# Low parts of split weights made by a negating copy and an accumulating transfer instead of a VectorE subtraction

## The chip, the core and the metric

The kernel runs on one core of a Trainium2 chip. A core has five engines that run at the same time, each with its own queue of instructions that it takes in order: TensorE (PE in the profile; its weight loads are PEld), VectorE (DVE), ScalarE (ACT), GpSimd (POOL) and SyncE (SP), which here only issues DMA transfers. Sixteen DMA engines move data between DRAM and the on-chip memory. The metric is the device time of one execution in microseconds (us); the median of three runs of the kernel before is 1519.1 us (1518.18 to 1520.67).

## What is computed

One block of a streaming encoder on 512 tokens of 1024 features, in float32: two SwiGLU feed-forwards around a mixer, and a last norm.

```python
x = x + 0.5 * swiglu(rms_norm(x, n1), ffn1_w_in, ffn1_w_out)      # 1024 -> 2*2816 -> 1024
h = rms_norm(x, nm)
b, c, xa, z, xbc, dt, ga, gb = split(h @ w_in)
y_a = (b * conv3(c * xa)) @ short_w_out
xs, bm, cm = split(silu(conv4(xbc) + bias))                       # 32 heads in 8 groups
y_b = group_norm((ssd_scan(xs, dt, bm, cm) + xs * D) * silu(z)) @ ssm_w_out
x = x + (sigmoid(ga) * y_a + sigmoid(gb) * y_b) @ w_out
x = x + 0.5 * swiglu(rms_norm(x, n2), ffn2_w_in, ffn2_w_out)
return rms_norm(x, nf)
```

Nearly all the arithmetic is in the matrix products with the weights. Their precision comes from splitting each factor into two float32r numbers, a high part and a low part.

## The kernel before

**Blocks of weights.** All weights are read once from DRAM, as 260 blocks in the order of their use (`src`, lines 82 to 107). A block has 128 partitions and as a rule 8 K-tiles of 128 columns (1024 float32 values in each partition, 512 KB); the third block of each output tile of a feed-forward has 6 K-tiles, the three blocks `wz0` of the first group have 3, 3 and 2 K-tiles of 288 columns.

**prep()** (lines 110 to 127) makes the next block ready. SP loads it into a tile `wraw` (two buffers, line 121). ScalarE copies `wraw` to `wh`, rounding to float32r: the high part (line 125). VectorE subtracts `wh` from `wraw` into `wl`: the low part (line 126). `wh` and `wl` have three buffers each.

**take()** (line 131) gives the oldest ready block to its user and calls prep() for one more, so that two blocks are being prepared or stand ready while one is in use. A block's `wh` and `wl` go into the buffers of the block three before it, so its preparation can't begin before TensorE has finished with that block.

**The main stream.** `mm3` (line 158) multiplies a block with the activations, which are split as well: for each K-tile three matmuls, high weights with high activations (line 164), high with low (165), low with high (166). The low part of a block is thus first needed by its third matmul. TensorE's order is written out by hand: after each K-tile `sq.tick()` puts in the small matmuls of the mixer that are due (class Order). The order on the other engines is left to the Tile framework, which also places all semaphores.

**Stages.** First feed-forward: 44 blocks of input weights, 24 of output weights. Mixer: 8 groups. A group projects C (a block), then B and two blocks x0, x1 (each followed by a convolution on VectorE and SiLU on ScalarE, `conv_silu`, line 369, which begins with a small memset on GpSimd, L371), and z through `gate` (line 301), which keeps its blocks for four token tiles: in group 0 the three blocks `wz0`, in the others two blocks at the end of the group. The first group also has the chain for dt (`dt_chain`, line 337) on VectorE. The scan of a group puts many small operations on all engines: `steps` (GpSimd, L471), `weights` (matmul L480, exp L483, VectorE L484), `within` (L493), `states` (matmul L453, VectorE L460 and L463), `across` (L504), the gated norm (L515 to L529, with GpSimd L510 and L527). Matmul L409 is the first one of `inner`, once in each group. Then come the merge gates, the SSD output projection, the short convolution, its projection, `w_out`, and the second feed-forward. The last output tile of all is done in two halves of the tokens (lines 679 to 692), so that its six blocks are each used for half the usual time, and the norm of the first half runs beside the second half's products.

Of the kernel before, what the change touches and what calls it, by code (L numbers as in the profile page):

```python
# [12 lines left out]
F32 = mybir.dt.float32  # L13
F32R = mybir.dt.float32r
AF = mybir.ActivationFunctionType
ALU = mybir.AluOpType
# [13 lines left out]
NC = T // P  # L30
EPS = 1e-5

# columns of the packed per-feature parameters
PF_N1, PF_NM, PF_N2, PF_NF = 0, 8, 16, 24
PF_SC = 32
PF_CW = 56
# [3 lines left out]


class Order:
    """The order of the tensor engine's work: the main stream advances in ticks (a K-tile of a
    projection each); what depends on other engines is put in so many ticks later."""

    def __init__(self):
        self.now = 0
# [22 lines left out]
def hybrid_block(ctx: ExitStack, tc: tile.TileContext, xT, w1i, w1o, wmx, wz0, wso, wsso,  # L70
# [7 lines left out]
    ctx.enter_context(tc.manual_schedule(engines={mybir.EngineType.PE}))  # L78
    sq = Order()

# [1 line left out]
    src = []  # L82
    src += [(w1i[i], KT) for i in range(2 * FT)]
    kcut = [(0, 8), (8, 16), (16, FT)]
# [23 lines left out]
    ready = []  # L108

    def prep():  # L110
        """The next block of weights as two float32r parts whose sum is exact."""
        if not src:
            return
        ap, _ = src.pop(0)
        n = ap.shape[-1]
        raw = wp.tile([P, D], F32, tag="wraw", name="wraw", bufs=2)
        cuts = [slice(0, n)]
        if len(src) == NSRC - 1:
            cuts = [slice(0, n // 2), slice(n // 2, n)]
        for h in cuts:  # L120
            nc.sync.dma_start(raw[:, h], ap[:, h])
        wh = wp.tile([P, D], F32R, tag="wh", name="wh")
        wl = wp.tile([P, D], F32R, tag="wl", name="wl")
        for h in cuts:
            nc.scalar.copy(wh[:, h], raw[:, h])  # L125
            nc.vector.tensor_tensor(wl[:, h], raw[:, h], wh[:, h].bitcast(F32), ALU.subtract)  # L126
        ready.append((wh, wl))

    NSRC = len(src)
# [3 lines left out]
        prep()  # L133
        return w

# [1 line left out]
    xall = pers.tile([P, KT, T], F32, name="xall")  # L137
    xr = [xall[:, j, :] for j in range(KT)]
    pf = pers.tile([P, PF_W], F32, name="pf")
# [11 lines left out]
    def col(i):  # L151
        return pf[:, i : i + 1]

# [1 line left out]
    def bank(tag="mm"):  # L155
        return ps.tile([P, T], F32, tag=tag, name=tag, bufs={"mm": 3, "sg": 2}.get(tag, 1))

    def mm3(out, w, xs, first=True, last=True, tk=slice(0, T)):
        """out += w.T @ x over the K-tiles xs, both in pairs of parts, for the tokens tk."""
        wh, wl = w  # L160
        n = len(xs)
        for i, xk in enumerate(xs):
            sl = slice(i * P, (i + 1) * P)
            nc.tensor.matmul(out, wh[:, sl], xk[:, 0, tk], start=first and i == 0, stop=False)  # L164
            nc.tensor.matmul(out, wh[:, sl], xk[:, 1, tk], start=False, stop=False)  # L165
            nc.tensor.matmul(out, wl[:, sl], xk[:, 0, tk], start=False, stop=last and i == n - 1)  # L166
            sq.tick()
# [9 lines left out]
        nc.vector.tensor_tensor(dst[:, 1, :], s, dst[:, 0, :].bitcast(F32), ALU.subtract)  # L177

    class Norm:
        """RMS norm of the residual: the parts of x * gain, and 1 / RMS per token, which the  # L180
        products are scaled by afterwards."""

        def __init__(self, gain):
            self.gain = gain
# [85 lines left out]
                nc.scalar.activation(xr[m], xr[m], AF.Copy, scale=col(PF_NF + m))  # L270
        return hid

# [1 line left out]
    n1 = Norm(PF_N1)  # L274
    prep()
    n1.parts(0)
# [17 lines left out]
    ffn(n1, nm, ("mm", "mm", "mm", "py", "po", "tr"))  # L294
    nm.later(5, 11)

# [1 line left out]
    xw = nm.xw  # L298
    CH = NC * HEADS

    def gate(zw, wide, c0, cn):
        """z of a group for the token blocks c0 .. c0 + cn, tokens on the partitions."""
        pz = bank()
        for c in range(c0, c0 + cn):
            o = pz[:, (c - c0) * wide : (c - c0 + 1) * wide]
            tk = slice(c * P, (c + 1) * P)
            step = -(-KT // len(zw))
            for k in range(KT):
                wh, wl = zw[k // step]
                sl = slice(k % step * wide, (k % step + 1) * wide)  # L310
                nc.tensor.matmul(o, xw[k][:, 0, tk], wh[:, sl], start=k == 0, stop=False)  # L311
                nc.tensor.matmul(o, xw[k][:, 0, tk], wl[:, sl], start=False, stop=False)  # L312
                nc.tensor.matmul(o, xw[k][:, 1, tk], wh[:, sl], start=False, stop=k == KT - 1)  # L313
                if k % 2 == 1:
                    sq.tick()
        return pz
# [18 lines left out]
                                       pr[:, 0:HEADS], ALU.mult, ALU.add)  # L335

    def dt_chain():
        # softplus(v) = max(v, 0) + log1p(exp(-|v|)), log1p(e) = 2 atanh(e / (2 + e))
        nc.vector.scalar_tensor_tensor(e, v, -1.0, v, ALU.mult, ALU.min)
        nc.scalar.activation(e, e, AF.Exp)  # L340
        na = tp.tile([P, HEADS], F32, tag="na", name="na", bufs=1)
        nc.scalar.activation(na, pr[:, HEADS : 2 * HEADS], AF.Exp)
        nc.vector.tensor_scalar(s, e, 2.0, None, ALU.add)
        nc.vector.reciprocal(s, s)
        nc.vector.tensor_tensor(s, s, e, ALU.mult)
        nc.vector.tensor_tensor(s2, s, s, ALU.mult)
        nc.vector.tensor_scalar(pl, s2, 2.0 / 17, 2.0 / 15, ALU.mult, ALU.add)
        for q in (13, 11, 9, 7, 5, 3, 1):
            nc.vector.tensor_tensor(pl, pl, s2, ALU.mult)
            nc.vector.tensor_scalar(pl, pl, 2.0 / q, None, ALU.add)  # L350
        nc.vector.tensor_tensor(pl, pl, s, ALU.mult)
        nc.vector.scalar_tensor_tensor(dt, v, 0.0, pl, ALU.max, ALU.add)
        nc.vector.scalar_tensor_tensor(av, dt, -1.0,
                                       na.unsqueeze(1).broadcast_to([P, NC, HEADS]),
                                       ALU.mult, ALU.mult)
        nc.vector.tensor_copy(ah, av)
        nc.vector.tensor_tensor(al, av, ah.bitcast(F32), ALU.subtract)

    def decays():
        """exp of the sums of a within a chunk: up to a token, after it, and of all."""  # L360
        pe = bank("sg")
        for i, m in enumerate((tri, mgt_r.bitcast(F32), ones)):
            nc.tensor.matmul(pe[:, i * CH : (i + 1) * CH], m, av.rearrange("p c h -> p (c h)"),
                             start=True, stop=True)
        nc.scalar.activation(dec.rearrange("p i c h -> p (i c h)"), pe[:, : 3 * CH], AF.Exp)
        nc.vector.tensor_tensor(dtd, dt, ds, ALU.mult)

    def conv_silu(o, pt, ft):
        """Scale, causal convolution over 4 taps, bias and SiLU of one 128-channel tile."""
        xp = tp.tile([P, T + 3], F32, tag="ta", name="xp")  # L370
        nc.gpsimd.memset(xp[:, 0:3], 0.0)  # L371
        nc.vector.tensor_tensor(xp[:, 3:], pt, nm.rb, ALU.mult)
# [11 lines left out]
        return act.tile(shape, dtype, tag="act", name=name, bufs=FT)  # L384

    class Group:
        """One group of the SSD mixer: 4 heads that share B and C."""

        def __init__(self, g):
            self.g = g  # L390
# [5 lines left out]
            self.st = [None] * NC  # L396

        def heads(self, apx):
            """Values of the group's heads, each over its 64 channels."""
            n = apx.shape[1]  # L400
            return apx[:, :, self.hs].unsqueeze(3).broadcast_to([P, n, HG, HD])

        def inner(self):
            """C B^T within the chunks, [s, l], and B with tokens on the partitions."""
            pc = bank("sg")
            pb = bank("tr")
            for c in range(NC):
# [40 lines left out]
                ALU.mult)  # L448

        def states(self, c):  # L450
            """State that enters chunk c + 1: what chunk c adds and the decayed one before."""
            pst = bank("po")
            nc.tensor.matmul(pst[:, :GC], self.btk[:, c, :], self.xdd[:, c, :],  # L453
                             start=True, stop=True)
# [9 lines left out]
            self.st[c + 1] = sn  # L464

        def steps(self, c):
            """a of chunk c masked to the tokens up to l, [t, head, l], in two parts."""
            self.au[c] = []
            for part in (ah.bitcast(F32), al):
                au = tp.tile([P, HG, P], F32R, tag="td", name="au", bufs=3)  # L470
# [3 lines left out]
                self.au[c].append(au)  # L474

        def weights(self, c):
            """exp(sum of a over (s, l]) * C B^T of chunk c, [s, head, l]."""
            sgp = bank("sg")
            for i in range(2):
                nc.tensor.matmul(sgp, mgt_r, self.au[c][i].rearrange("p h l -> p (h l)"),  # L480
# [5 lines left out]
            self.ex[c] = ex  # L486

        def within(self, c):
            # two heads wide: head h's part lies at 128 h, the last one's at 128 h + 64
            py = bank("py").rearrange("p (h l) -> p h l", l=P)  # L490
            for h in range(HG):
                d0 = min(h * HD, GC - P)
# [88 lines left out]
                pz = gate(zw, GC, c0, 2)  # L581
                gate_out(pz, G.zs, GC, c0, 2)

    # gates of the merge, then the SSD output projection
    mb = []
    for j in range(KT):
        pt = project(xw)
# [15 lines left out]
            mm3(pt, take(), ys[i * KT : (i + 1) * KT], i == 0, i == 1)  # L603
        nc.vector.tensor_tensor(mb[m], pt, mb[m], ALU.mult)

    # short gated convolution
    ya = []
    for j in range(KT):
        pc = project(xw)
# [39 lines left out]
        n2.parts(m)  # L649
        n2.square(m)  # L650

# [1 line left out]
    n2.later(5, 11)  # L653
    nf = Norm(None)
    hid = ffn(n2, None)
    # the last feature tile in halves of the tokens: the first half's norm and output run
    # beside the second half's products
    m = KT - 1
    nf.last = tp.tile([P, T], F32, tag="td", name="nlast", bufs=3)

# [32 lines left out]


def blocks(w, mw=P):
    """[K, M] -> [M / mw, P, K / P * mw]: the K-tiles of each block of mw columns side by side."""
    k, m = w.shape
    return w.reshape(k // P, P, m // mw, mw).transpose(2, 1, 0, 3).reshape(m // mw, P, k // P * mw)


def feat(v):
    """[n, F] per-feature rows -> [P, F / P * n], feature tile by feature tile."""
    n, f = v.shape
    return v.reshape(n, f // P, P).transpose(2, 1, 0).reshape(P, f // P * n)

# [52 lines left out]
```

## Time and profile before

| | us |
|---|---|
| median of three runs | 1519.1 |
| the profiled execution: first to last instruction (span) | 1517.2 |
| TensorE busy | 1492.1 |
| VectorE busy | 830.2 |
| ScalarE busy | 533.9 |
| GpSimd busy | 267.3 |

The median stands 1.9 us above the profiled execution's span. Busy time is the union of an engine's instructions; DMA issues and waits don't count. In a row of the timeline come the start in us from the span's beginning, the duration in us, engine, line, operation, output<-inputs, shapes, a count, and in brackets the engine's idle time before it with what ended it. A row of grouped instructions ends with busy us, mean ns of one, and idle us before them. A row of a line's durations gives minimum/median/maximum in ns. A row of waits gives us in total, times, longest us. PEclk is TensorE's granted clock, 1.00 being full speed.

### The profile page before, as it was taken

What the parts mean: (1) busy time and instruction counts of PE and PEld (TensorE: products, weight loads), DVE (VectorE), ACT (ScalarE), POOL (GpSimd) and SP (SyncE); (2) the same over time, 40 slices, a digit from 0 to 9 for tenths busy, and PEclk for the clock granted to TensorE, in tenths of its full rate; (3) what the DMA queues carried; (4) which work ended last, traced back from release to release, by engine and by line L of the source; (5) the groups of instructions that cost most, each with busy time, mean ns of one, the idle gap of its engine ahead of it and who ended that gap; (6) DMA issues with size and microseconds to landing.
All of it is one profiled execution on the core that took longest, in us unless ns stands there. A gap on an engine that the chain in (4) does not pass through costs nothing.

```text
span 1517.2 us, 17880 instructions
## 1 busy us (share of the span) xinstructions
PE 1492.1 (98%) x7214; PEld 1255.7 (83%) x7214; DVE 830.2 (55%) x990; ACT 533.9 (35%) x721; POOL 267.3 (18%) x236
## 2 busy tenths in 40 slices
PE   7999999999999999999999999999999999999997
PEld 6888888888878888888988888888888888888887
DVE  5545454323797877888754246654454545453223
ACT  5323222222455555445542122223243323232232
POOL 0111111000045442344300001111121111110011
PEclk9999999999999999999999999999999999999998
DMA  5333333323221221222222233333222222223233
GB/s 178 98 97 98 97 97 91 104 87 98 84 70 53 73 68 59 84 70 70 70 84 97 97 98 97 98 97 98 97 97 95 87 103 91 102 93 104 87 104 105
DMA packets 41539, 139.48 MB, mean 92 GB/s; under 512 B 4592, under 2 KB 7024, under 8 KB 41456
## 3 DMA queue, kind: packets, MB, share of 16 engines
q1 hardware_dynamic: 41456, 138.34, 28.7%
q8 instruction: 57, 0.93, 0.2%
q14 instruction: 26, 0.21, 0.0%
HBM read 136.22 MB, written 2.10 MB: 91 GB/s over the span
## 4 chain that ended last, share of the span: by engine, by line
PE 90%; DVE 5%; issue 3%; ACT 1%; DMA 0%; POOL 0%; SPq 0%; POOLq 0%; DVEq 0%; ACTq 0%
PE mm L166 27%; PE mm L164 27%; PE mm L165 27%; PE py L493 1%; PE mm L313 1%; PE mm L312 1%; PE mm L311 1%; DVE ex L484 1%; DVE wl L126 1%; PE po L504 1%; DVE xdd L437 1%; DVE cv L376 1%; PE sg L212 0%; ACT L483 0%; PE po L453 0%
## 5 line engine op out<-in xcount | busy, mean ns | idle before, releaser
L125 ACT CAST wh<-wraw 128x1024 fp32r<-128x1024 f32 (+3 forms) x261 | 269.6, 1033 | 715.9 <-PE mm L165 655.9
L164 PE MATMUL mm<-xw,wh 128*128 128x512 f32 x1256 | 503.2, 401 | 7.6 <-ACT wh L125 5.7
L126 DVE TENSOR_TENSOR wl<-wraw,wh 128x1024 fp32r<-128x1024 f32 (+3 forms) x261 | 394.2, 1511 | 199.7 <-ACT wh L125 198.5
L166 PE MATMUL mm<-xw,wl 128*128 128x512 f32 x1256 | 491.3, 391 | 0.3 <-DVE wl L126 0.3
L165 PE MATMUL mm<-xw,wh 128*128 128x512 f32 x1256 | 491.1, 391 | 0.0
L164 PEld LDWEIGHTS mm<-xw,wh 128*128 128x128 f32 x1256 | 237.0, 189 | 55.4 <-ACT wh L125 5.7
L166 PEld LDWEIGHTS mm<-xw,wl 128*128 128x128 f32 x1256 | 236.8, 189 | 51.6 <-DVE wl L126 1.4
L165 PEld LDWEIGHTS mm<-xw,wh 128*128 128x128 f32 x1256 | 237.2, 189 | 48.5 <-DVE xw L192 0.8
L164 PE MATMUL mm<-hk,wh 128*128 128x512 f32 (+1 forms) x374 | 141.1, 377 | 0.0
L165 PE MATMUL mm<-hk,wh 128*128 128x512 f32 (+1 forms) x374 | 140.8, 377 | 0.0
L166 PE MATMUL mm<-hk,wl 128*128 128x512 f32 (+1 forms) x374 | 140.8, 376 | 0.0
L250 POOL TENSOR_TENSOR hf<-sg,tu 128x512 f32<-128x512 f32 x44 | 58.6, 1331 | 401.9 <-ACT wh L125 343.2
L248 DVE TENSOR_TENSOR tu<-mm,rb 128x512 f32<-128x512 f32 x42 | 29.0, 691 | 134.6 <-PE mm L166 134.6
L165 PEld LDWEIGHTS mm<-hk,wh 128*128 128x128 f32 x374 | 70.4, 188 | 13.0
L164 PEld LDWEIGHTS mm<-hk,wh 128*128 128x128 f32 x374 | 70.4, 188 | 12.9
L166 PEld LDWEIGHTS mm<-hk,wl 128*128 128x128 f32 x374 | 70.4, 188 | 12.8
L376 DVE SCALAR_TENSOR_TENSOR cv<-xp,pf,cv 128x512 f32<-128x512 f32 x96 | 74.9, 780 | 1.2
L311 PE MATMUL mm<-wh,xw 128*128 128x256 f32 (+1 forms) x256 | 75.2, 294 | 0.0
L312 PE MATMUL mm<-wl,xw 128*128 128x256 f32 (+1 forms) x256 | 72.7, 284 | 0.0
L313 PE MATMUL mm<-wh,xw 128*128 128x256 f32 (+1 forms) x256 | 72.7, 284 | 0.0
L244 DVE TENSOR_TENSOR tg<-mm,rb 128x512 f32<-128x512 f32 x43 | 29.7, 691 | 67.8 <-PE mm L166 64.2
L203 POOL TENSOR_TENSOR nacc<-nacc,nsq 128x512 f32<-128x512 f32 x18 | 26.4, 1468 | 223.5 <-ACT nsq L201 223.5
(181 smaller groups left out, 1670.5 us busy)
## 6 DMA issues: line engine op xcount, KB each, us to landing
wraw<-wmx SPq DMA_DIRECT2D x86, 512.0 KB, 3.5
wraw<-w2i SPq DMA_DIRECT2D x44, 512.0 KB, 3.2
wraw<-w1i SPq DMA_DIRECT2D x43, 512.0 KB, 3.5
wraw<-w2o SPq DMA_DIRECT2D x18, 512.0 KB, 3.5
wraw<-w1o SPq DMA_DIRECT2D x16, 512.0 KB, 3.5
wraw<-wsso SPq DMA_DIRECT2D x16, 512.0 KB, 3.7
wraw<-wso SPq DMA_DIRECT2D x8, 512.0 KB, 3.2
wraw<-wmo SPq DMA_DIRECT2D x8, 512.0 KB, 3.3
```

What stands on the lines that cost most here:

```text
L125: nc.scalar.copy(wh[:, h], raw[:, h])
L126: nc.vector.tensor_tensor(wl[:, h], raw[:, h], wh[:, h].bitcast(F32), ALU.subtract)
L164: nc.tensor.matmul(out, wh[:, sl], xk[:, 0, tk], start=first and i == 0, stop=False)
L165: nc.tensor.matmul(out, wh[:, sl], xk[:, 1, tk], start=False, stop=False)
L166: nc.tensor.matmul(out, wl[:, sl], xk[:, 0, tk], start=False, stop=last and i == n - 1)
L244: nc.vector.tensor_tensor(tg, pg, nrm.rb, ALU.mult)
L248: nc.vector.tensor_tensor(tu, pu, nrm.rb, ALU.mult)
L250: nc.gpsimd.tensor_tensor(hf, sg, tu, ALU.mult)
L311: nc.tensor.matmul(o, xw[k][:, 0, tk], wh[:, sl], start=k == 0, stop=False)
L312: nc.tensor.matmul(o, xw[k][:, 0, tk], wl[:, sl], start=False, stop=False)
L313: nc.tensor.matmul(o, xw[k][:, 1, tk], wh[:, sl], start=False, stop=k == KT - 1)
L376: nc.vector.scalar_tensor_tensor(cv, xp[:, q : q + T], col(PF_CW + 4 * ft + q), cv, ALU.mult, ALU.add)
```

## The change

For all blocks but the first four, `wl` is no longer `wraw - wh` on VectorE. ScalarE writes the negated high part straight from `wraw` (Copy with scale -1.0, rounded to float32r in the output) into `wl`, then copies `wraw` to `wh` as before. Then a transfer that GpSimd issues reads the same block from DRAM a second time and adds it to `wl` in place. Loads by SP, buffers and TensorE's order stay. The diff also empties comment and docstring lines, which is left out here.

```diff
         wh = wp.tile([P, D], F32R, tag="wh", name="wh")
         wl = wp.tile([P, D], F32R, tag="wl", name="wl")
-        for h in cuts:
+        if len(src) >= NSRC - 4:
+            for h in cuts:
+                nc.scalar.copy(wh[:, h], raw[:, h])
+                nc.vector.tensor_tensor(wl[:, h], raw[:, h], wh[:, h].bitcast(F32), ALU.subtract)
+        else:
+
+            h = cuts[0]
+            nc.scalar.activation(wl[:, h], raw[:, h], AF.Copy, scale=-1.0)
             nc.scalar.copy(wh[:, h], raw[:, h])
-            nc.vector.tensor_tensor(wl[:, h], raw[:, h], wh[:, h].bitcast(F32), ALU.subtract)
+            nc.gpsimd.dma_start(wl[:, h], ap, accum_op=ALU.add)
         ready.append((wh, wl))
```

## The prediction

> **What bounds the kernel now.** I read the page's head, the busy time in stretches of 50 us, TensorE's waits, its clock, the timeline.
>
> ```profile
> span 1517.2 us, 17880 instructions
> PE 1492.1 (98%) x7214; PEld 1255.7 (83%) x7214; DVE 830.2 (55%) x990; ACT 533.9 (35%) x721; POOL 267.3 (18%) x236
> ...
> 150.00:200.00 50.00, 50.00 (x223) 41.38 (x222) 24.41 (x23) 15.12 (x19) 5.18 (x4) 1.00 0.32 104
> 400.00:450.00 50.00, 46.49 (x228) 38.40 (x227) 47.72 (x78) 26.73 (x31) 17.25 (x18) 0.97 0.25 74
> ```
>
> TensorE is the bound: in a stretch of the feed-forward (first numbers of a row: stretch, PE busy) it is busy for 50.00 of 50.00 us, with VectorE at half load. A VectorE operation taken out there gains nothing. Only in the mixer, above all where its first groups meet (400 to 470 us), does TensorE wait, and there VectorE is busy for 47.72 of 50 us. The waits in groups 0 to 1, then those in the later groups:
>
> ```profile
> PE po L453 <- DVE xdd L437: 1.9, 1, 1.9
> PE sg L409 <- ACT ex L483: 1.5, 1, 1.5
> PE sg L480 <- POOL au L471: 1.3, 1, 1.3
> PE po L453 <- ACT st L458: 0.5, 1, 0.5
> ...
> PE po L453 <- DVE st L463: 3.5, 5, 0.7
> ```
>
> The first waits also cost clock. PEclk, the number after the five engines' busy times, is 0.50 in two stretches of 3.41 us:
>
> ```profile
> 440.74:444.15 3.41, 3.41 (x14) 3.13 (x14) 3.41 (x5) 1.20 (x1) 0.00 (x0) 0.50 0.27 53
> 468.04:471.45 3.41, 3.41 (x10) 2.64 (x9) 3.41 (x3) 2.97 (x4) 2.21 (x2) 0.50 0.02 5
> ```
>
> The same matmul of successive groups shows the sum of it:
>
> ```profile
> 440.70 2.07 PE L409 MATMUL sg<-cb 128*128 128x128 f32 x8 [1.46 <-ACT ex L483]
> ...
> 496.12 0.89 PE sg L409 x8
> ...
> 541.52 0.89 PE sg L409 x8
> ```
>
> From group 1 to 2 it takes 496.12 - 440.70 = 55.4 us, from 2 to 3 only 45.4: 10.0 us lost. Ahead of 440.70 the waits of 1.3, 0.5 and 1.5 us lost 3.3 more. With the 3.5 us of the later groups, 16.8 us are the most that the change can win.
>
> **What it removes.** 256 subtractions on VectorE.
>
> ```profile
> L125 ACT CAST wh<-wraw 128x1024 fp32r<-128x1024 f32 (+3 forms) x261 | 269.6, 1033 | 715.9 <-PE mm L165 655.9
> L126 DVE TENSOR_TENSOR wl<-wraw,wh 128x1024 fp32r<-128x1024 f32 (+3 forms) x261 | 394.2, 1511 | 199.7 <-ACT wh L125 198.5
> ...
> 514.91 2.91 DVE L126 TENSOR_TENSOR wl<-wraw,wh 128x1024 fp32r<-128x1024 f32 x1
> ...
> 518.92 2.06 DVE L126 TENSOR_TENSOR wl<-wraw,wh 128x1024 fp32r<-128x1024 f32 x1
> ...
> 521.30 0.41 DVE L463 TENSOR_TENSOR st<-po,st 128x256 f32<-128x256 f32 x1
> ...
> 521.76 0.70 PE L453 MATMUL po<-xdd,btk 128*128 128x256 f32 x2 [0.69 <-DVE st L463]
> ```
>
> VectorE loses 256 x 1.51 = 387 us, of which TensorE sees only what stands before its waits. In a later group two subtractions (2.91 and 2.06 us) run shortly ahead of the L463 that TensorE waits for by 0.69 us; without them it is there in time, so I take the whole 3.5 us. In groups 0 to 1 VectorE has no pause, each 1.5 us block comes off its backlog, and the waits for ACT and POOL there stand behind late VectorE results; I take 12 of the 13.3 us, since the dt chain stays. Gain: 15.5 us. Late next are ScalarE, with one more operation per block, and GpSimd.
>
> **What it adds.** A block's `wl` is now ready after a negating copy, a GpSimd issue and a transfer, in place of a cast and a subtraction.
>
> ```profile
> L125 ACT CAST wh<-wraw x261: 617/1053/1066, 5.0 to 1496.5; 128x1024 fp32r<-128x1024 f32 x119, 128x768 fp32r<-128x768 f32 x9, 128x512 fp32r<-128x512 f32 x1, 128x864 fp32r<-128x864 f32 x1
> L191 ACT ACTIVATE xw<-xall,pf x24: 705/718/727, 4.2 to 1142.2; 128x512 fp32r<-128x512 f32 x24
> ```
>
> *Negation.* The scaled Copy of 512 columns takes 0.72 us, the cast of 512 columns 0.62 (the minimum), so 1024 columns take 1.05 + 0.1 = 1.15 us. ScalarE gets 256 x 1.15 = 294 us and goes from 534 to 828 of 1517: not a bound. `wh` comes 1.15 us later than before, before which two blocks are still in work.
>
> *Issue on GpSimd.* No row shows a DMA issued by GpSimd. Near rows:
>
> ```profile
> 395.01 0.33 SPq L121 DMA_DIRECT2D wraw<-wmx  x1
> ...
> L217 POOL TENSOR_TENSOR rt<-ms,nhalf x5: 696/1012/1025, 29.0 to 1507.8; 128x4 f32<-128x4 f32 x3, 128x2 f32<-128x2 f32 x2
> ...
> L445 POOL TENSOR_TENSOR y<-xt,pr 128x1024 f32<-128x1024 f32 x8 | 19.2, 2406 | 0.0
> ```
>
> The bounds are SP's issue, 0.33 us, and the longest GpSimd operation, 2.4 us; I take 1.0, what GpSimd takes for four columns, its price for any instruction. 256 such issues lie in GpSimd's 1250 idle us.
>
> *Transfer.*
>
> ```profile
> q1 hardware_dynamic: 41456, 138.34, 28.7%
> ...
> wraw<-wmx SPq DMA_DIRECT2D x86, 512.0 KB, 3.5
> ...
> wraw<-wz SPq DMA_DIRECT2D x1, 288.0 KB, 2.6
> ```
>
> A plain block lands 3.5 us after its issue. 28.7% of 1517 us for 138.34 MB, that is 264 blocks of 0.524 MB, is 1.65 us of all 16 engines per block. An accumulating transfer also reads its destination; I count that as a second 1.65 us, so 5.15 us (bounds: 3.5 if the add is free; 7.0 if everything doubles). The engines then have 1.65 + 3.3 = 4.95 us of work per block.
>
> From ScalarE's start to `wl`: 1.15 + 1.0 + 5.15 = 7.3 us; bounds 1.15 + 0.33 + 3.5 = 5.0 and 1.15 + 2.4 + 7.0 = 10.55.
>
> The Trainium skill, "DMA: Bandwidth & Descriptors", section on the anatomy of a GpSimd DMA, fits such a transfer as 2.0 us plus its bytes at 436 GB/s: 3.2 us for 512 KB, near the row's 3.5. Its page "Collectives: The Full Stack", in the bandwidth ceiling's account of ReduceScatter, says that an add costs a second source read and no more. By both, an estimate is 2.0 + 2 x 1.2 = 4.4 us with the issue, 5.55 from ScalarE's start, and the costs below would be about 5 us and the time about 1509. The trace of before has no such transfer to check it by.
>
> **Where it is hidden.** Feed-forward:
>
> ```profile
> 155.98 1.06 ACT L125 CAST wh<-wraw 128x1024 fp32r<-128x1024 f32 x1 [3.86 <-PE mm L165]
> ...
> 166.86 1.05 ACT L125 CAST wh<-wraw 128x1024 fp32r<-128x1024 f32 x1 [3.86 <-PE mm L165]
> ...
> 167.29 0.39 PE L166 MATMUL mm<-xw,wl 128*128 128x512 f32 x1
> ```
>
> ScalarE starts on a block when the buffer comes free, two blocks ahead; the block's first low-part matmul comes 167.29 - 155.98 = 11.3 us later. 7.3 us fit, even 10.55. The start two blocks on, 166.86, gives TensorE's pace: 5.44 us per block, above the 4.95 us of DMA work. A transfer waiting for its negation on GpSimd's queue holds up only `hf` (L250), whose inputs come later. If the cover went, each us would cost 1 us per two blocks.
>
> **Where it isn't.** Three places have less lead:
>
> ```profile
> 380.84 0.67 ACT L125 CAST wh<-wraw 128x576 fp32r<-128x576 f32 x1 [5.10 <-issue]
> ...
> 384.19 0.29 PE L312 MATMUL mm<-wl,xw 128*128 128x288 f32 x1
> ...
> 392.67 2.25 ACT L125 CAST wh<-wraw 128x1024 fp32r<-128x1024 f32 x2 [0.77 <-PE mm L313]
> ...
> 395.03 0.50 PE L166 MATMUL mm<-xw,wl 128*128 128x512 f32 x1
> ...
> 1491.07 1.05 ACT L125 CAST wh<-wraw 128x1024 fp32r<-128x1024 f32 x1 [0.58 <-PE mm L165]
> ...
> 1496.27 0.28 PE L166 MATMUL mm<-hk,wl 128*128 128x256 f32 x1
> ```
>
> - Group 0, third `wz0` block (288 KB): 0.77 + 1.0 + 2.6 + 0.9 = 5.3 us from 380.84 is 386.1, needed at 384.19: 2.0 us (bounds 0.3 and 5.0).
> - Group 0, block B: the gate holds all three buffers to its end. 392.67 + 7.3 = 400.0, needed at 395.03: 4.9 us (2.6 and 8.2). So long a wait will halve the clock once for 3.41 us as above: 1.7 more.
> - The tail, where blocks last half as long: 1491.17 + 7.3 = 1498.5, needed at 1496.27: 2.2 us (0 and about 7 over the following blocks).
>
> Cost: 2.0 + 4.9 + 1.7 + 2.2 = 10.8 us. Net: 10.8 - 15.5 = -4.7 us. The profiled 1517.2 becomes 1512.5, and with the 1.9 us around it 1514.4: I say **1515 us**.
>
> **Rivals.**
> *Cheap add.* With the low bounds the cost is 0.3 + 2.6 = 2.9 us, and all 16.8 are won: about 1505. For it: the engines are 71% idle now, so a second stream has room.
> *Half the gain.* ScalarE, in the chain that runs to L483 in each group, gets 1.15 us more per block and takes half the gain: 1519.1 + 10.8 - 8 = 1522. Against: no later group shows TensorE waiting for ScalarE.
> *GpSimd's queue* (slower). It is in order, and it stands still for other reasons:
>
> ```profile
> POOL xp L371 <- DVE cv L376: 121.0, 29, 16.3
> ...
> 538.61 1.06 ACT L125 CAST wh<-wraw 128x1024 fp32r<-128x1024 f32 x1 [3.28 <-PE mm L165]
> ...
> 548.21 0.28 PE L312 MATMUL mm<-wl,xw 128*128 128x256 f32 x1
> ```
>
> A transfer queued behind such a memset is issued 121.0 / 29 = 4.2 us later on average: 11.5 us in all. The second z block of a group (in group 3: ScalarE from 538.6, the low part's buffer free 0.2 us later, used at 548.21) has 9.4 us, so 2.1 us are lost in each of 7 groups, 15 in all: 1530. It decides from a delay of 2 us on. For it: GpSimd also loses 1 us per block to the issues. Against: VectorE is freed, so the memsets wait less.
> *Engines full* (slower). If the add takes three times the plain 1.65 us, a block needs 6.6 us of the DMA engines against TensorE's 5.44, and about 210 blocks outside the mixer's groups lose 1.16 each: 1519 + 245 = 1764. It decides from 3.8 us per accumulated block (2.3 times plain). Nothing in the trace excludes it.
> *Not what it says:* fewer than 256 transfers by GpSimd; nothing speaks for it.
>
> **How the numbers follow.** Forecast 0.45 (its own range 1509 to 1522: of this, 0.30 faster, 0.13 same, 0.02 slower); cheap add 0.12, faster; half the gain 0.16 (0.07 same, 0.09 slower); GpSimd's queue 0.15 (0.02 same, 0.13 slower); engines full 0.12, slower. Within 0.2% (3 us) is what a measurement of this kernel can't tell from no change. Faster 0.42, same 0.22, slower 0.36. The range goes from 1503, just under the cheap add, to the high bounds of the three places without any gain, 1519 + 5.0 + 8.2 + 1.7 + 7 = 1541, rounded up to 1545; it leaves out the full engines.
>
> **What would show it.** Right: VectorE near 445 us busy, ScalarE near 825, a second DMA queue of about 132 MB; groups 1 to 2 apart by 46 us; TensorE waiting at L312 and L166 near 384 and 395 us for a DMA, again near 1497, nowhere in the feed-forwards. Issue to landing should be near 6 us with the issue. Wrong: waits for `wl` in every block (engines full), or in z blocks behind memsets on GpSimd (its queue), or no shorter group 1 (the gain).

## The result, and the profile after

The changed kernel takes 1541.5 us (median of four runs, 1539.4 to 1542.5), the kernel before 1518.6 beside it: a ratio of 1.0145, 95% interval 1.0132 to 1.0157. It is slower by 22.9 us, where 4 us faster was forecast. The profiled execution, the fastest of the four, has a span of 1537.7 us, 20.5 more than before.

The page's head and the queues (packets, MB, share of the 16 DMA engines) of the changed kernel:

```profile
span 1537.7 us, 18465 instructions
PE 1498.2 (97%) x7214; PEld 1259.5 (82%) x7214; DVE 473.5 (31%) x734; ACT 772.1 (50%) x977; POOL 463.8 (30%) x492
...
q0 software_dynamic: 36864, 131.61, 48.5%
q1 hardware_dynamic: 41456, 138.34, 31.5%
```

The work moved as the diff says: VectorE lost 357 us, ScalarE got 238, GpSimd 196.5 (its 256 issues, 0.88 us each, count as busy in this profile), and a second queue carries 131.61 MB. TensorE is still busy for 97%, with the same 7214 matmuls. So the loss has to be looked for in its waits (us in all, times, longest) and its clock. In the changed kernel all lines behind prep() stand 7 further down (L166 is now L173, L312 is L319, L409 is L416):

```profile
PE mm L173 <- DMA wl<-wmx: 5.9, 1, 5.9
PE mm L173 <- DMA wl<-w2o: 3.9, 4, 2.8
PE mm L319 <- DMA wl<-wz: 3.8, 1, 3.8
PE sg L416 <- ACT ex L490: 2.8, 1, 2.8
PE po L460 <- DVE xdd L444: 2.0, 1, 2.0
PE mm L319 <- DMA wl<-wmx: 1.9, 2, 1.6
PE mm L173 <- DMA wl<-wsso: 0.9, 1, 0.9
```

Five of the seven rows are low parts that have not landed: third z block and block B of group 0, the tail (2.8 of the 3.9), the SSD projection, last z blocks of groups. The two others are waits of group 1 that the change was meant to shorten; the row for ScalarE even grew, from 1.5 to 2.8. The five waits of L453 in the later groups are gone. Two stretches of group 0 in the view by stretches (PEclk is the eighth entry, behind the five engines' times):

```profile
391.35:394.76 3.41, 3.41 (x17) 3.41 (x16) 0.25 (x1) 0.75 (x2) 0.00 (x0) 0.50 0.00 0
405.00:415.24 10.24, 6.06 (x14) 4.79 (x15) 3.37 (x11) 3.37 (x4) 0.86 (x1) 0.50 0.97 224
```

The first long wait, for the third z block, runs from 386.80 to 390.58 us, and the clock is at half for 3.41 us behind it. The second, for block B, runs from 403.29 to 409.18 us; the clock falls to half 1.7 us into this wait and stays there for 10.24 us, 6.06 of them behind the wait. TensorE works 3.41 and 6.06 us at half speed, which loses 1.7 + 3.0 = 4.7 us. Two more stretches of 3.41 us, at 483.51 us (group 2) and 1510.92 us (the last six blocks), cost 1.7 us each.

By stage, from the first matmul of a stage's first block to that of the next one's, in us; the columns from "no add" on are experiments told below:

| stage | before | changed | no add | no loads | groups only |
|---|---|---|---|---|---|
| first feed-forward and what precedes it | 373.6 | 375.7 | 373.4 | 374.2 | 373.6 |
| group 0 | 38.75 | 53.55 | 38.73 | 48.93 | 38.75 |
| group 1 | 55.53 | 53.66 | 52.32 | 54.60 | 53.97 |
| group 2 | 46.96 | 47.51 | 45.31 | 46.03 | 46.90 |
| groups 3 to 7 | 227.17 | 224.73 | 222.17 | 222.30 | 222.38 |
| gb to the second feed-forward's 7th output tile | 746.1 | 748.2 | 746.0 | 747.0 | 746.2 |
| last six blocks to the end | 29.07 | 34.30 | 28.24 | 31.11 | 28.30 |

Group 0 alone loses 14.8 us, the last six blocks 5.2, both feed-forwards and the SSD projection some 4; the groups 1 to 7 win 3.8 together.

How late a low part is can be read off any block of the first feed-forward. Rows of the changed kernel's timeline:

```profile
156.82 1.05 ACT L132 CAST wh<-wraw 128x1024 fp32r<-128x1024 f32 x1 [2.91 <-PE mm L172]
157.78 1.05 ACT L131 ACTIVATE wl<-wraw 128x1024 fp32r<-128x1024 f32 x1
159.13 0.88 POOL L133 DMA_DIRECT2D wl<-w1i  x1
168.14 0.39 PE L173 MATMUL mm<-xw,wl 128*128 128x512 f32 x1
```

and its DMA issues (median us from issue to landing at the end):

```profile
wl<-wmx POOLq DMA_DIRECT2D x86, 512.0 KB, 7.6
...
wl<-w1i POOLq DMA_DIRECT2D x40, 512.0 KB, 7.7
...
wraw<-w1i SPq DMA_DIRECT2D x43, 512.0 KB, 6.0
```

The buffer of `wl` is free at 157.0 (the last L173 of its old block), but in ScalarE's queue the cast of the same block stands first, as it does for 231 of the 256 blocks, and the negation starts 0.8 us late. It takes 1.05 us, the issue comes 0.3 us later at 159.13, and with the median landing of 7.7 us the block would be there at 166.8: 9.8 us after the buffer was free, 1.3 us ahead of its first use at 168.14 (this one took 8.0 us and was 1.0 us ahead). The plain loads slowed down as well, from 3.5 to 6.0 us for `w1i`. A lead of 11.2 us holds that; 9.8 us, in the output projections, holds it narrowly and not for every block, 9.4 to 9.6 us, at the last z blocks, hardly.

### The profile page after: what moved, and what is told of

It is laid out like the page before. It is cut to its first block, busy times and chain, and to the rows that moved or that the text cites. A ratio compares the mean times of both kernels' runs of the same rounds, so it can differ in the third digit from the quotient of the medians.

```text
span 1537.7 us, 18465 instructions
## 1 busy us (share of the span) xinstructions
PE 1498.2 (97%) x7214; PEld 1259.5 (82%) x7214; DVE 473.5 (31%) x734; ACT 772.1 (50%) x977; POOL 463.8 (30%) x492
## 3 DMA queue, kind: packets, MB, share of 16 engines
q0 software_dynamic: 36864, 131.61, 48.5%
q1 hardware_dynamic: 41456, 138.34, 31.5%
## 4 chain that ended last, share of the span: by engine, by line
PE 85%; issue 6%; DMA 4%; DVE 2%; ACT 1%; POOL 1%; SPq 0%; POOLq 0%; ACTq 0%; DVEq 0%
PE mm L173 25%; PE mm L172 25%; PE mm L171 25%; DMA wl<-wmx 2%; PE py L500 2%; PE mm L319 1%; PE mm L320 1%; PE mm L318 1%; DMA wl<-w2o 1%; PE sg L487 1%; PE po L460 1%; POOL wl L133 1%; PE po L511 1%; ACT wl L131 1%; DMA wl<-w1o 1%
## 5 line engine op out<-in xcount | busy, mean ns | idle before, releaser
L132 ACT CAST wh<-wraw 128x1024 fp32r<-128x1024 f32 (+2 forms) x256 | 264.9, 1035 | 570.2 <-PE mm L172 478.2
L173 PE MATMUL mm<-xw,wl 128*128 128x512 f32 x1256 | 493.1, 393 | 5.9 <-DMA wl<-wmx 5.9
L173 PEld LDWEIGHTS mm<-xw,wl 128*128 128x128 f32 x1256 | 237.3, 189 | 57.5 <-DMA wl<-wmx 7.1
L131 ACT ACTIVATE wl<-wraw 128x1024 fp32r<-128x1024 f32 (+2 forms) x256 | 265.3, 1036 | 16.9 <-PE mm L319 5.5
L173 PE MATMUL mm<-hk,wl 128*128 128x512 f32 (+1 forms) x374 | 142.3, 380 | 4.3 <-DMA wl<-w2o 3.9
L133 POOL DMA_DIRECT2D wl<-wmx x86 | 77.1, 897 | 177.6 <-ACT wl L131 170.4
L173 PEld LDWEIGHTS mm<-hk,wl 128*128 128x128 f32 x374 | 71.1, 190 | 19.5 <-DMA wl<-w2o 4.9
L319 PE MATMUL mm<-wl,xw 128*128 128x256 f32 (+1 forms) x256 | 74.1, 289 | 5.8 <-DMA wl<-wz 3.8
L271 DVE SCALAR_TENSOR_TENSOR xall<-mm,xall 128x512 f32<-128x512 f32 x15 | 10.4, 691 | 195.5 <-PE mm L173 195.5
```

Of the source, the lines that this page charges most:

```text
L131: nc.scalar.activation(wl[:, h], raw[:, h], AF.Copy, scale=-1.0)
L133: nc.gpsimd.dma_start(wl[:, h], ap, accum_op=ALU.add)
```

## The experiments

My theory after this: the accumulating transfer is long because it shares the 16 DMA engines with the next block's plain load, so that a latency of some 9 us meets leads of 9 to 11 us almost everywhere and much shorter ones in group 0 and the tail; and the gain in group 1 wasn't there to be had. Rivals: the waits are only moved from stage to stage, the addition itself takes that long, or ScalarE's second pass ate the gain.

**1. Group 0 as before.**

```diff
-        if len(src) >= NSRC - 4:
+        i = NSRC - 1 - len(src)
+        if i < 4 or 69 <= i <= 74:
```

> The six blocks z0, z1, z2, B, x0 and x1 of group 0 (numbers 69 to 74) get VectorE's subtraction back, all other blocks stay as in the changed kernel. Theory: the 14.8 us by which group 0 grew (38.75 to 53.55 us) are the waits of 4.5 us at L318 and 6.3 us at L172 for the late low part and the half clock that followed; then group 0 is back near 39 us, L319 and L173 do not wait there, and the time is 1541.5 - 14.8 = 1527 us (1524 to 1530). Rival: the lateness is only moved on, since the groups behind inherit the work of VectorE and ScalarE that the wait gave room for; then group 0 falls, group 1 grows by most of it, and the time stays over 1534 us.

(The waits meant are those of L319 and L173, 3.8 and 5.9 us in the view of waits.)

Measured: 1526.5 us (1525.8 to 1529.2), 15.0 less than the changed kernel; group 0 takes 39.3 us, 14.3 less, and group 1 53.65 as in the changed kernel. By the medians nothing was moved on: six blocks cost two thirds of the loss. (The profiled execution here is the slowest of its four, and its span is only 10.3 us shorter: from group 3 on its stages take 4.8 us more than the changed kernel's.) What is left in the groups shows in its waits (lines one further down):

```profile
PE sg L417 <- ACT ex L491: 2.8, 1, 2.8
...
PE mm L320 <- DMA wl<-wmx: 2.4, 6, 0.6
```

The second row is the last z block of six groups, late by 0.4 us each time on average.

**2. The tail as before.**

```diff
-        if len(src) >= NSRC - 4:
+        if len(src) >= NSRC - 4 or len(src) < 9:
```

> The last nine blocks get VectorE's subtraction back, the rest stays as in the changed kernel. Theory: the 5.2 us by which the last six blocks to the end grew (29.07 to 34.30 us), and the 0.6 us of the stage before, are waits for the transfer in blocks that are in use for only half the time; the time is 1541.5 - 5.5 = 1536 us (1535 to 1538). Rival: the end is late because of the clock or of the last norm, not of the low parts: the time stays within 1.5 us of 1541.5.

Measured: 1533.1 us (1531.8 to 1533.9), 8.4 less: more than expected. The last six blocks take 28.29 us, 6.0 less than in the changed kernel, and the spans differ by 6.4. The rest of the 8.4 us stands between the medians alone, since the changed kernel's profiled execution was its fastest.

**3. No addition, and 4. no low part at all.** How much was there to win?

```diff
-            nc.gpsimd.dma_start(wl[:, h], ap, accum_op=ALU.add)
```

> The accumulating transfer is left out, the negating copy stays, so the low part of the weights holds minus the high part and the products are not the reference's. No low part can be late for a transfer. Theory on record: VectorE's subtraction cost 15.5 us in the groups, so the time is 1518.6 - 15.5 = 1503 us (1501 to 1506). Rival: ScalarE's second pass takes most of that back in the groups, as the changed kernel's group 1 (55.5 to 53.7 us) hints: only 4 to 6 us are won, 1513 to 1515 us, and TensorE still waits for ScalarE at L416 (the first matmul of inner).

```diff
-            nc.scalar.activation(wl[:, h], raw[:, h], AF.Copy, scale=-1.0)
...
-            nc.gpsimd.dma_start(wl[:, h], ap, accum_op=ALU.add)
+            wl = wh
```

> Neither negating copy nor transfer: the high part is used in the place of the low part from the fifth block on, so the products are not the reference's. This is what the removal of VectorE's subtraction can bring at no cost at all. Theory on record: 1503 us (1501 to 1506), and the same as without the transfer alone, since ScalarE is no bound. Rival (ScalarE's second pass eats the gain): 1501 to 1506 here, but 8 us or more below the kernel that leaves out the transfer alone. Second rival (the subtraction cost little): 1513 us or more in both.

Measured: 1508.0 us (1507.8 to 1508.9) without the addition, 1508.8 (1507.2 to 1509.6) without the negation too, before 1518.0. So ScalarE's second pass costs nothing that can be measured, and the whole gain of taking 256 subtractions off VectorE is 10.0 us, not 15.5. Both the theory on record (1503) and the rival with ScalarE (8 us between the two) fall. Part of the gain is clock, too: the kernel before lost 1.7 us in each of its two half-clock stretches, at 440.74 and 468.04 us. Experiment 3 has none in the groups; experiment 4 has one, at 463.62 us, and its group 2 takes 46.8 us where that of experiment 3 takes 45.3. Why is group 1 not shorter still? A stretch of 10 us about its end in the kernel before, and without the addition (PE, PEld and DVE are the second to fourth entries; by then the second kernel is 3 us further on in its work):

```profile
460.00:470.00 10.00, 8.08 (x51) 7.17 (x50) 9.34 (x8) 7.46 (x12) 9.51 (x7) 0.90 0.00 0
```

```profile
460.00:470.00 10.00, 8.12 (x49) 6.94 (x49) 9.58 (x10) 8.92 (x11) 7.23 (x5) 1.00 0.31 96
```

VectorE is as full without the subtractions, and there were next to none here in the kernel before either: its rows of L126 in these 10 us last 0.02 and 0.05 us. VectorE does the first scans' own operations. And TensorE's two long waits of group 1 (1.5 us ahead of L409 and 1.9 for `xdd` in the kernel before) are still there without the addition:

```profile
PE sg L415 <- ACT ex L489: 2.2, 1, 2.2
PE po L459 <- DVE xdd L443: 1.9, 1, 1.9
```

Half of the 10.0 us by which group 1 is longer than group 2 is no loss at all. The groups of TensorE's lines in the kernel before, first between 440.70 and 496.12, then between 496.12 and 541.52 us:

```profile
L493 PE MATMUL py<-xdt,ex 128*128 128x128 f32 x56 | 7.5, 276 | 0.3 <-DVE y L498 0.3
L504 PE MATMUL po<-st,cb 128*128 128x256 f32 x12 | 3.3, 387 | 0.1
```

```profile
L493 PE MATMUL py<-xdt,ex 128*128 128x128 f32 x32 | 4.2, 274 | 0.0
...
L504 PE MATMUL po<-st,cb 128*128 128x256 f32 x6 | 1.6, 378 | 0.0
```

Group 1 holds 24 more matmuls of `within` and 6 more of `across`, 5.0 us together: the end of group 0's scan, which TensorE has to do in any case. Another 3.4 us are the two half-clock stretches, and only the rest, some 1.6 us, is waiting and small things. Without the addition, and without those stretches, the two pitches are 51.0 and 44.4 us, still 6.6 apart.

**5. The transfer without the plain loads, and 6. without the addition.** Is it the company or the adding that makes it long?

```diff
-        raw = wp.tile([P, D], F32, tag="wraw", name="wraw", bufs=2)
+        if len(src) >= NSRC - 4:
+            raw = wp.tile([P, D], F32, tag="wraw", name="wraw", bufs=2)
+            keep.append(raw)
+        else:
+            raw = keep[-1]
...
-            nc.sync.dma_start(raw[:, h], ap[:, h])
+            if len(src) >= NSRC - 4:
+                nc.sync.dma_start(raw[:, h], ap[:, h])
```

> SyncE's loads stop after the fourth block; every later block casts and negates the fourth block's stale data, and the accumulating transfer runs alone, so the products are not the reference's. Theory (the transfer and the next plain load share the 16 DMA engines): alone it lands 5.4 to 5.7 us after its issue, as the few blocks of the changed kernel did that met no load, in place of 7.6; the waits for low parts outside group 0 (1.3 + 1.5 + 0.6 us) and in the groups go, those of group 0 (8.6 us less 2 each) and of the tail shrink by about 2 us each: 1541.5 - 3 - 7 - 4 = 1527 us (1521 to 1531). Rival (the addition itself takes 7.6 us, whatever else runs): landing and time stay, 1538 to 1542.

```diff
-            nc.gpsimd.dma_start(wl[:, h], ap, accum_op=ALU.add)
+            nc.gpsimd.dma_start(wl[:, h], ap.bitcast(F32R))
```

> The same transfers by GpSimd, of the same bytes to the same place, but writing instead of adding, so the low part holds the whole weight and the products are not the reference's. If the addition is what makes the transfer long: issue to landing falls from 7.6 us to about 4 (3.5 as SyncE's loads before, and GpSimd's slower issue), the queue's share of the DMA engines from 48.5% to about 31%, and the time to 1541.5 - 10 - 5 - 7 = 1520 us (1513 to 1525). Rival (a second stream of 132 MB and GpSimd's issue make it long, the addition is free): landing over 6.5 us, share over 42%, 1536 to 1542.

Measured: 1525.6 us (1524.7 to 1527.3) without loads, 1519.6 (1518.1 to 1520.7) with a plain transfer. (Without loads the two parts still sum to the weight, to the rounding of the low part, whatever the high part is: the expectation was wrong to say otherwise.) Queue and landing without loads:

```profile
q0 software_dynamic: 36864, 131.61, 51.1%
...
wl<-wmx POOLq DMA_DIRECT2D x86, 512.0 KB, 5.4
```

its waits, where L179 is block B and L325 the third z block of group 0:

```profile
PE mm L179 <- DMA wl<-wmx: 3.8, 1, 3.8
...
PE mm L325 <- DMA wl<-wz: 2.7, 1, 2.7
```

and the plain transfer beside the loads:

```profile
q1 hardware_dynamic: 41456, 138.34, 28.6%
q0 software_dynamic: 36864, 131.61, 24.8%
...
wraw<-wmx SPq DMA_DIRECT2D x86, 512.0 KB, 3.6
wl<-wmx POOLq DMA_DIRECT2D x86, 512.0 KB, 4.6
```

A plain GpSimd transfer lands in 4.6 us and leaves the loads at 3.6 us (3.5 before). With the addition, alone, it takes 5.4 us and twice the engines' time: 51.1% of 1524.1 = 779 us against 24.8% of 1518.9 = 377. Addition and loads together: 7.6 us, and the loads 4.5 to 6.6. So neither rival alone is right: the addition doubles the transfer's work on the engines, and this work then collides with the loads, for another 2.2 us. By the spans, the collision costs 1537.7 - 1524.1 = 13.6 us. The Trainium skill, "DMA: Bandwidth & Descriptors", section on SWDGE, HWDGE and iDMA, says that both kinds of queue feed the same DMA engines, which take them in turn; both streams slowing down in the changed kernel agrees with that.

**7. First use later.** In each block TensorE takes the 8 matmuls with the low part last.

```diff
+        seq = [(k, p) for k in range(n) for p in (0, 1, 2)]
+        if cur[0] not in (0, 1, 2, 3, 68, 189):
+            seq = [(k, p) for k in range(n) for p in (0, 1)] + [(k, 2) for k in range(n)]
```

> All as in the changed kernel, but in each projection block (not the first four, not C of group 0, not the first of the second feed-forward) TensorE takes the 8 low-weight matmuls after the 16 with the high part, so a low part is first needed 3.5 us later (1.75 in the tail's half blocks) at the same work. Theory (a fixed latency of 8.6 to 9 us against a lead of 9.4 to 11.2): the waits of the output projections and of the SSD projection go, B of group 0 waits 2.8 in place of 6.3 us and the tail loses at most 2; z2 of group 0 and the last z blocks stay, as their order is another: 1541.5 - 1.3 - 0.6 - 1.5 - 3.5 - 4 = 1530.5 us (1526 to 1533). Rival (the DMA engines are full, so that a wait that is moved comes back): 1538 to 1542.

Measured: 1527.7 us (1526.3 to 1531.5), with the 512 KB transfers landing in 7.4 to 8.1 us (7.0 to 7.7 in the changed kernel). Its waits (L176 is mm3, L324 the gate):

```profile
PE mm L324 <- DMA wl<-wz: 3.6, 1, 3.6
PE mm L324 <- DMA wl<-wmx: 3.2, 6, 1.2
...
PE mm L176 <- DMA wl<-wmx: 2.7, 1, 2.7
...
PE mm L176 <- DMA wl<-w2o: 0.5, 1, 0.5
```

B of group 0 waits 2.7 us, not 5.9, and the output projections take the times of before (119.68 and 104.72 us). In these blocks a wait that is moved by 3.5 us doesn't come back, so the DMA engines are loaded but not full; it is a latency. The last z blocks, whose order is as it was, wait more than in the changed kernel (3.2 us in place of 1.9), and groups 3 to 7 take 226.6 us in place of 224.7; why was not looked into.

**8. to 10. A version that keeps the gain.** Low-part matmuls last, and VectorE's subtraction for six blocks of group 0 and the last z block of each later group; then the same with the last nine blocks as before; then the order alone, without any transfer.

```diff
-        if len(src) >= NSRC - 4:
+        i = NSRC - 1 - len(src)
+        if i < 4 or 69 <= i <= 74 or i in range(80, 117, 6):
```

> The order of the run before (low-weight matmuls last) with VectorE's subtraction kept in group 0 (z1, z2, B, x0, x1 and z0) and in the last z block of each later group; the accumulating transfer for the other 243 blocks. Theory: what leaving out all low-part work is worth, 10 us (1518.0 to 1508.0), is nearly all kept and no low part is late: 1510 us (1508 to 1513), under both kernels. Rival (transfers slow SyncE's loads and GpSimd's own work in the groups, so that part of the gain is lost anyway): 1514 to 1518 us.

Measured: 1513.5 us (1512.6 to 1514.7), ratio 0.9968 (0.9956 to 0.9981): faster than before, but not by what was expected. The groups win what they should; the last six blocks take 32.97 us. ScalarE and TensorE there:

```profile
1491.19 0.83 ACT L134 CAST wh<-wraw 128x768 fp32r<-128x768 f32 x1 [3.43 <-DMA wraw<-w2o]
1491.93 0.84 ACT L133 ACTIVATE wl<-wraw 128x768 fp32r<-128x768 f32 x1
1492.67 0.40 ACT L698 ACTIVATE nlast<-xall 128x256 f32<-128x256 f32 x1
...
1493.12 0.71 PE L225 MATMUL sg<-cst,nlast 128*128 128x128 f32 x4 [2.50 <-ACT nlast L698]
```

A late load holds up ScalarE's cast for 3.43 us, the square of the norm stands behind it in ScalarE's queue, and TensorE waits for that, 2.5 us, and then works for 3.41 us at half clock, which loses another 1.7.

```diff
+        if i < 4 or 69 <= i <= 74 or i > 250 or i in range(80, 117, 6):
```

> The selected version with its last nine blocks as in the kernel before (VectorE's subtraction, low-weight matmuls not last). Theory: the selected version lost 3.9 us to the kernel before in its last six blocks to the end (32.97 against 29.07 us), because ScalarE's square of the last tile stood behind a negation that waited for a late load; without this the tail is 28.3 us and the time 1513.5 - 4.7 = 1509 us (1507.5 to 1511). Rival (the tail is slow for the order of its matmuls or a changed clock): 1511.5 to 1514.

Measured: 1510.9 us (1510.1 to 1511.5), ratio 0.9947 (0.9934 to 0.9959); the last six blocks take 28.31 us. This run changes transfer and order together in the last nine blocks, so the time alone doesn't part the two; that the load was the cause rests on the rows above.

> The kernel before with the low-weight matmuls last (not in the last nine blocks); VectorE's subtraction everywhere, no transfer. It tells whether the selected versions owe their time to the order alone. Theory: no low part is late in the kernel before outside the groups, so the order is worth nothing: 1516.5 to 1520, level with before. Rival (the order itself relieves the groups): 1508 to 1513.

Measured: 1518.7 us (1517.1 to 1520.1), ratio 0.9996 (0.9986 to 1.0005): the order by itself is worth nothing.

**11. The source in the on-chip memory.**

```diff
-            nc.gpsimd.dma_start(wl[:, h], ap, accum_op=ALU.add)
+            nc.gpsimd.dma_start(wl[:, h], raw[:, h], accum_op=ALU.add)
```

> The accumulating transfer takes its source from the loaded tile in place of DRAM, so a block is read from DRAM once; the tile is then held until the transfer has landed, and the next load but one can't start before. Theory (what fills the engines is the addition, twice a plain transfer's time whatever the source; and loads that wait for it collide less or come late): the queue's share stays at 45 to 51%, landing 5.4 to 7.6, time 1530 to 1550. Rival (the second read of DRAM is what costs): share near 25 to 35%, landing under 5 us, time under 1525.

Measured: 1661 us (1652 to 1675), ratio 1.094, far above what I had expected. Its queue, landing and the waits for loads:

```profile
q0 software_dynamic: 36864, 131.61, 43.3%
...
wl<-wraw POOLq DMA_DIRECT2D x236, 512.0 KB, 5.2
```

```profile
ACT wh L132 <- DMA wraw<-wmx: 175.7, 39, 7.8
```

43.3% of 1673.3 us is 725 us of the engines: the addition costs them about the same from either source, so the second read of DRAM isn't what is dear. The time comes from the buffer. `wraw` is held until the transfer has landed, so cast and negation (2.0 us), wait and transfer (0.3 + 5.2) and the load of the block after next (4.2) follow one another: 11.7 us for two blocks that TensorE uses in 10.9. Which part each of them has in the 120 us more was not taken apart further.

**12. Only where VectorE is short.** The transfer for 35 blocks, in groups 1 to 7 without their last z blocks; TensorE's order as before.

```diff
-        if len(src) >= NSRC - 4:
+        i = NSRC - 1 - len(src)
+        if not 75 <= i <= 116 or i in range(80, 117, 6):
```

> The transfer only in groups 1 to 7, without the last z block of each: 35 blocks; everywhere else VectorE's subtraction, TensorE's order as in the kernel before. Theory (only in the groups does TensorE see VectorE's load): groups 1 to 7 gain what they gained in the selected versions, 2.65 + 0.9 + 4.8 us, and nothing is lost elsewhere: 1519 - 8.3 = 1511 us (1509 to 1513), level with the version that changes 237 blocks. Rival (part of the selected versions' gain came from the order of the matmuls or from the other blocks, since VectorE and ScalarE come to the groups less laden): 1514 to 1518.

Measured: 1511.8 us (1511.5 to 1512.3), ratio 0.9955 (0.9942 to 0.9969). 18.35 MB go through GpSimd's queue in place of 131.61, and two thirds of the possible gain is kept, most of what 234 blocks brought (6.8 of 8.4 us). Of the groups, 3 to 7 win 4.8 us and 1 wins 1.6, about the half-clock stretch at 440.74 us, which this run hasn't. Its 35 transfers land in 7.6 us too, although their queue has only 7.0% of the engines' time: by this and experiment 5 the latency goes with the load that runs beside a transfer, not with the queue's mean share.

## Why the prediction was wrong

Its sum against what the runs showed, in us of the profiled spans (the costs against the kernel without the addition, by the stage table; the terms are rounded):

| term | predicted | measured |
|---|---|---|
| gain on VectorE | -15.5 | -11.1 |
| third z block of group 0 | +2.0 | +3.8 |
| block B of group 0 | +4.9 | +5.9 |
| half clock in group 0 | +1.7 | +4.7 |
| the rest of group 0 | 0 | +0.4 |
| tail | +2.2 | +6.1 |
| groups 1 to 7 | 0 | +6.1 |
| both feed-forwards and the SSD projection, the start | 0 | +4.5 |
| sum | -4.7 | +20.5 |

By size, the places that were put at nothing account for 10.6 us of the difference, group 0 for 6.2, the gain for 4.4 and the tail for 3.9. That the measured time lies between 1503 and 1545 us all the same is luck: the top was 21.9 us of costs at three places and no gain, and measured were 31.5 us of costs, a third of them at other places, less a gain of 11.

**The failed step: the time from a free buffer to `wl`, taken as 7.3 us and hidden everywhere but at three places; above all its term for the transfer's landing.** "I count that as a second 1.65 us, so 5.15 us" from the end of the issue. As work of the engines this was right: 48.5% of 1537.7 us for 251 blocks of 0.524 MB is 2.97 us per block, 3.3 was predicted, and with the plain load (31.5%, 264 blocks) it is 4.8 us against 4.95. As a latency it was wrong, since a transfer that shares busy engines takes longer than alone. Alone it lands 5.4 us after the start of its issue, less than the 1.0 + 5.15 of the prediction; beside the loads in 7.6. The prediction had the number that should have warned it, 4.95 us of work in 5.44 us, and used it only to ask whether the engines are full, not how long a transfer then takes. The high bound, 7.0 + 2.4 for landing and issue, does hold 7.6.

**From free buffer to `wl`:** 7.3 us predicted, 9.8 measured: 0.8 for the cast that goes ahead of the negation, 1.05 for the negation (1.15), 0.3 until GpSimd takes up the issue, 7.6 with the issue (6.15). The first and the third were not in the sum. "Hidden in feed-forward" held for blocks with a lead of 11.2 us, by 1.3 at the median. With the 9.8 us of the output projections (one of the blocks in work there has only six K-tiles) it held narrowly, and a few blocks waited, 0.4 us at most in the first. The last z blocks of the groups, which the prediction had priced only under GpSimd's queue, have 9.4 to 9.6 us, and one of them waited 1.6. The late block of the SSD projection had 11.3 us, and its transfer took only 5.7; its negation started 5.2 us after the buffer was free, behind casts of `yh` on ScalarE.

**Group 0** waited at the two places and nearly for the times that were named; 8.6 us became 14.8, through 1.8 + 1.0 us longer waits, 3.0 us more of half clock (two stretches, 3.41 and 10.24 us, in place of one of 3.41) and 0.4 of small change. That a long wait halves the clock "once" was read from two rows; the runs below show that a wait's length alone doesn't settle it. **The tail** lost 6.1 in place of 2.2: its blocks are in use for half the time, the largest wait there was 2.8 us at a lead of 7.2, and one half-clock stretch (1.7) belongs to it. Of the 6.1 us of groups 1 to 7, too, 1.7 are a half-clock stretch, the one in group 2 that the kernel without the addition hasn't.

**The gain** was too large by 4.4 us in the spans. "10.0 us lost" from the pitch of L409 took TensorE's own work for a loss: 5.0 us of it are more matmuls, and 3.4 the half clock. "Each 1.5 us block comes off its backlog" was little to stand on: in group 1 of the kernel before (412.31 to 467.84 us) all subtractions together take 6.9 us of VectorE. Of the waits in group 1, that for `xdd` did not move (1.9 and 2.0 us), and the one before L409 grew from 1.5 to 2.8 in the changed kernel. In groups 3 to 7 the gain was larger than said, 5.0 us against 3.5; the 1.65 us of group 2 are the half clock at 468.04 us.

Two small readings of the prediction are off as well. The tail's cast starts at 1491.07 us, not 1491.17, so 2.2 should be 2.1. And 1.0 us isn't GpSimd's "price for any instruction": its memsets of three columns (L371) take 0.13 us on average, the issue took 0.88.

**The rivals.** "Cheap add" falls even with an add that costs nothing: with the plain transfer the span is 12.8 us longer than without a transfer (1518.9 against 1506.1), where 2.9 were priced. "Engines full" decided from 3.8 us of the engines per accumulated block; 2.97 were measured, and the waits that the later first use took away in the projection blocks did not come back. "GpSimd's queue" named the right blocks, the z blocks of the groups, but for the wrong reason: all seven of their transfers are issued 0.3 us after the negation, none stands behind a memset, and they are late by the landing. Other blocks of the groups did stand in GpSimd's queue, B in groups 3 to 7 for 2.9 us and z of group 1 for 4.7, but none of these came late to TensorE. The price was 6.1 us for all of groups 1 to 7, not 15. "Half the gain" had ScalarE in the chain; leaving its pass out changes nothing measurable (1508.0 and 1508.8). What the prediction says of the Trainium skill's figures, "DMA: Bandwidth & Descriptors", anatomy of a GpSimd DMA, gave 4.4 us as an estimate with a second read; 5.4 us alone and 7.6 beside the loads were measured, so here it was too low, and so was its plain transfer (3.2 against 4.6 us beside the loads; alone it was not run).

## What to carry to other kernels

Work that moves from an engine that isn't the bound to a transfer is paid in latency: compare the whole time from free buffer to landing, under the traffic that will be there, with the lead of each kind of block, the shortest first. Before a longer stretch counts as lost time, count the matmuls in it and look at the clock. If only one stage is short of an engine, change only that stage's blocks: 35 of 256 brought 6.8 us, all of them cost 22.9.

## What the runs showed of the hardware

- An accumulating transfer into the on-chip memory takes the DMA engines twice as long as a plain one of the same bytes (779 against 377 us for 131.61 MB), from DRAM or from on-chip memory; 512 KB land in 5.4 us alone, 7.6 us beside plain loads, and those of 512 KB slow down from between 3.2 and 3.7 us to between 4.5 and 6.6. A plain transfer by GpSimd beside the same loads lands in 4.6 and slows most of them by 0 to 0.3 us.
- GpSimd is busy 0.88 us with an accumulating issue, 0.56 with a plain one.
- TensorE's clock goes to half for 3.41, 6.83 or 10.24 us, one, two or three times the same length, and the starts of such stretches in one run stand whole multiples of it apart: 405.00 - 391.35 = 13.65 = 4 x 3.41 and 483.51 - 405.00 = 78.5 = 23 x 3.41 in the changed kernel, 468.04 - 440.74 = 27.3 = 8 x 3.41 before. The wait's length alone doesn't set the loss. The wait of 5.9 us at block B comes with 10.24 us of half clock in the changed kernel and with 6.83 in experiment 2, in both from within the wait on; the wait for the third z block with 3.41 us in the changed kernel (3.8 us long) and with 6.83 in experiments 2 (3.3) and 7 (3.6); one of 1.5 us before L409 with 3.41 in the kernel before, one of 2.8 at the same place in experiment 12 with none.
